# Convolution stage: the norm's shift, the partial sums and a scale are read from PSUM, and three more column groups are split

## The chip, the core and the metric

The kernel runs on one core of a Trainium2 chip. The metric is the device time of one execution in microseconds (us). An execution comprises a little more than the span of the profile, which goes from the first to the last instruction.

## The reference

One Conformer block and one sparse-attention block with an expert layer follow each other on 256 tokens of width 2048, all in float32. The change touches the first stage of the first block and the last norm of the second:

```python
h = rmsnorm(x, norm1_g)                      # x: 256 x 2048
u = h @ w_in + b_in                          # 2048 -> 2 x 2048
val, gate = split(u, 2)
u = val * sigmoid(gate)
u = causal_dwconv(u, dw) + dw_b              # 31 taps, one filter for each channel
u = silu(layernorm(u, ln_g, ln_b))
y = u @ w_out + b_out
...
h = layer_norm(ALPHA * h + ffn, ln2_g, ln2_b)    # the last operation of all
```

and, lightly, the gates of the expert layer, which are summed by products of one-hot matrices.

## The kernel before

Activations lie channel-major: a tile is 128 channels x 256 tokens, 16 such tiles make the width of 2048. Tiles of PSUM are 128x512 float32, one bank each; the pool has two tags of four banks, `mm` (sums of the large products) and `aux` (everything else).

**The convolution stage** is the loop over `o` from 0 to 15 (lines 472 to 509), where `o` stands for 128 channels of `val` and the 128 of `gate` that belong to them. For each `o` TensorE makes a group of products into two `mm` banks, in one of two forms. `whole` (line 358) takes the float32 weights as they are; each product shows as two matmul records in the profile, so a group is 64 records of L363. `halves` (line 365) takes weights that were split into a rounded high half `whi` (ScalarE, L132) and a remainder `wlo` (in this stage GpSimd, L121), with three matmuls in place of the two records: L373 and L374 read `whi`, L375 reads `wlo`, 96 records in all. A split costs four chunks of ScalarE and four of GpSimd. The tiles `wraw` have five buffers, `whi` and `wlo` four each, which is one group. The constant `WHOLE` lists the `o` that take the first form; 0 and 1 are made from unscaled data (`gx`) and scaled afterwards.

Then `ev_conv(o)` adds the bias, applies the gate (ScalarE L387, VectorE L388) and writes `u`. `do_conv(o)` runs the 31 taps over it, and three engines share them. The first `npool` taps are multiplied on ScalarE (L406, L409) and added up on GpSimd (L410). For `o` = 15 twelve taps are matmuls with diagonal matrices (L417). The rest run on VectorE as multiply-add (L433, L437) into two accumulators that take turns, so that an instruction does not wait for the one just before it. Each accumulator lies in a bank of its own. Three additions join the parts: L438 (the two accumulators), L440 (GpSimd's part `p`), L442 (TensorE's part). `npool` comes from `NPOOL`: 9 for an `o` in `WHOLE`, 7 for the others, with values of their own for 0, 1 and 15. The loop calls `do_conv(o - 1)` between the products of `o` and `ev_conv(o)`.

**The shift of the norm.** Once four tiles are convolved, `Layer.first` sums them with a matrix of ones (L306), ScalarE copies the negative mean to the SBUF tile `nm` (L308), and VectorE adds it to these four tiles (L310). For `o` >= 4 the shift is put in as the addend of the second VectorE tap. ScalarE squares each tile (L238), GpSimd adds up tiles and squares (L231), and after `o` = 15 small matmuls (L244) sum over channels.

**The scale before the stage.** The RMS scale is spread over partitions by a matmul into `rps`, ScalarE copies it to SBUF (`rB`, L469), and VectorE forms the 16 tiles of `h` (L471) from `x` and this copy. VectorE and GpSimd share the splitting of `h` into `A` (L121), which the `halves` groups read.

**The last norm** (lines 1230 to 1246) does the 16 tiles in pairs of 128x512, a multiplication and a subtraction each (L1239), with scales that ScalarE copied from PSUM to SBUF (L1234). VectorE has the pairs below `FINAL_POOL`, GpSimd the rest; ScalarE applies gain and offset (L1245), VectorE does so for the two tiles of `FINAL_DVE` (L1242).

**The gates** (`gate_prep`, `gate_fire`): 64 of them, each four products. The last two (n >= `SPLIT_FROM`) have a first operand split in two halves.

The order of the instructions on an engine is that of a planner which takes the program's order as priority and may move an instruction ahead where its operands are expected earlier; `tc.keep_in_program_order` and `tc.issue_after` fix some places.

Of the kernel before, what the change touches and what calls it, by code (L numbers as in the profile page):

```python
# [10 lines left out]
F32 = mybir.dt.float32  # L11
F32R = mybir.dt.float32r
# [3 lines left out]
OP = mybir.AluOpType  # L16
AX = mybir.AxisListType

T = 256
# [9 lines left out]
NM = 4  # L29
NPOOL = {'X': 9, 'Y': 7, 0: 7, 1: 7, 15: 5}  # L30
NPE = {15: 12}
DIAG_AT = 13
EARLY = 1
NGX = 2
FINAL_POOL = 10
FINAL_ORDER = (0, 2, 10, 4, 6, 12, 8, 14)
FINAL_DVE = (8, 9)
APOOL = 2
WHOLE = (0, 1, 3, 5, 7, 9, 11, 13, 15)
GATES_AT = 16  # L40
SPLIT_FROM = 62
PER_UNIT = 2.3
# [11 lines left out]
def tile_body(ctx: ExitStack, tc: tile.TileContext, xT, vec, dw, w_ccin, w_ccout, w_m1, w_m2,  # L54
# [7 lines left out]
    work = ctx.enter_context(tc.tile_pool(name="work", bufs=2))  # L62
    psum = ctx.enter_context(tc.tile_pool(name="psum", bufs=4, space=bass.MemoryType.PSUM))
    dram = ctx.enter_context(tc.tile_pool(name="dram", bufs=1, space=bass.MemoryType.DRAM))
# [16 lines left out]
    def aux(shape=None, name="aux"):  # L81
        return psum.tile(shape or [128, 512], F32, name=name, tag="aux", bufs=4)

    def bank():
        return psum.tile([128, 512], F32, name="mm", tag="mm", bufs=4)

    def wk(name, shape=None, dtype=F32, bufs=2, tag=None):
        return work.tile(shape or [128, T], dtype, name=name, tag=tag or name, bufs=bufs)
# [24 lines left out]
    def col(v, i):  # L113
        return vc[:, v + i:v + i + 1]
# [177 lines left out]
    class Layer:  # L292
# [7 lines left out]

        def first(self, o, ap):
            self.tiles.append(ap)
            if o == NM - 1:
                self.ps = aux()
                for i, t in enumerate(self.tiles):
                    PE.matmul(self.ps[:, :T], ones, t, start=i == 0, stop=i == NM - 1)  # L306
                self.nm = wk("nm", bufs=1)
                ACT.activation(self.nm, self.ps[:, :T], AF.Copy, scale=-1.0 / (128 * NM))  # L308
                for t in self.tiles:
                    DVE.tensor_tensor(t, t, self.nm, OP.add)  # L310
                    self.st.add(t)
# [78 lines left out]
    def do_conv(o):  # L390
        if o == NM:
            for i in range(NM):
                ln.first(i, conv[:, i])
        u = us[o % 3]
# [18 lines left out]
        if npe:  # L413
            pe = aux()
            for i in range(npe):
                k = npool + i
                PE.matmul(pe[:, :T], diag[o][:, i], u[:, k:k + T], start=i == 0, stop=i == npe - 1)  # L417
        acc = [aux(), aux()]
        y = conv[:, o]
        k0 = npool + npe  # L420
        for k in range(k0, 31):
            i = (k - k0) % 2
            d = acc[i][:, :T]
            a, b = w(k)
# [11 lines left out]
            else:  # L436
                DVE.tensor_scalar(d, a, b, None, op0=OP.mult)  # L437
        DVE.tensor_tensor(y, acc[1 - (30 - k0) % 2][:, :T], y, OP.add)  # L438
        if npool > 1:
            DVE.tensor_tensor(y, y, p, OP.add)  # L440
        if npe:
            DVE.tensor_tensor(y, pe[:, :T], y, OP.add)  # L442
        if o >= NM:
            ln.rest(y, shifted=True)
# [25 lines left out]
    for kt in range(KT):  # L470
        DVE.scalar_tensor_tensor(h[:, kt], x[:, kt], col(V_G1, kt), rB, op0=OP.mult, op1=OP.mult)  # L471
    for o in range(NGX):
# [6 lines left out]
    for o in range(NGX, KT):  # L479
# [27 lines left out]
        if o < EARLY:  # L507
            do_conv(o - 1)
    do_conv(KT - 1)
    lo_eng[0] = [POOL, DVE]  # L510
    ln.finish()
# [570 lines left out]
    def gate_prep(n):  # L1082

        if n >= SPLIT_FROM:
            o = [pk("oh", [128, 4, 128], F32R, tag=f"oh{i}", bufs=1) for i in range(3)]
            t = slice(4 * n, 4 * n + 4)
            ghi = pk("ghi", [128, 4], F32R, bufs=2)
            glo = pk("glo", [128, 4], bufs=2)
            ACT.activation(ghi, R[:, 2, t], AF.Copy)
            sub(DVE, glo, R[:, 2, t], ghi)  # L1090
            for i in range(4):
                t = slice(4 * n + i, 4 * n + i + 1)
                DVE.tensor_scalar(o[0][:, i], iota, R[:, 0, t], ghi.bitcast(F32)[:, i:i + 1], op0=OP.is_equal, op1=OP.mult)
                DVE.tensor_scalar(o[1][:, i], iota, R[:, 0, t], glo[:, i:i + 1], op0=OP.is_equal, op1=OP.mult)
                DVE.tensor_scalar(o[2][:, i], iota, R[:, 1, t], None, op0=OP.is_equal)
            gates[n] = o
            return
        if not spare:
# [11 lines left out]
    def gate_fire(n):  # L1110
        if n % 8 == 0:
            gs.append(slot(4 + n // 8 % 2, [128, 128, 32], name="gs"))
        *o1, o2 = gates.pop(n)
        ps = aux(wide4)
        for i in range(4):
            for j, a in enumerate(o1):
                PE.matmul(ps[:, i], a[:, i], o2[:, i], start=j == 0, stop=j == len(o1) - 1)  # L1117
        t = 4 * (n % 8)
        ACT.activation(gs[-1][:, :, t:t + 4].rearrange("p c t -> p t c"), ps, AF.Copy)  # L1119
        if n % 8 == 7:  # L1120
            nc.gpsimd.dma_start(Gd[n // 8], gs[-1])
# [113 lines left out]
    for kt in FINAL_ORDER:  # L1235
        y = z[:, kt:kt + 2]
        eng = DVE if kt < FINAL_POOL else POOL
        for w, op in zip(wide, (OP.mult, OP.subtract)):
            tc.keep_in_program_order(eng.tensor_tensor(y, y, w[:, None].to_broadcast([128, 2, T]), op))  # L1239
# [85 lines left out]
```

## Time and profile before

| | us |
|---|---|
| median of 3 runs (lowest to highest) | 3055.45 (3045.72 to 3058.11) |
| profiled execution, its own time | 3056.73 |
| its span | 3054.9 |
| TensorE (PE in the rows) busy in it | 2997.2 (98%) |
| VectorE (DVE) busy | 2138.3 (70%) |
| ScalarE (ACT) busy | 1576.6 (52%) |
| GpSimd (POOL) busy | 458.3 (15%) |

PEld in the rows is TensorE's loading of weights, which runs beside its matmuls. TensorE is busy almost throughout, so the shares of the whole span say little on a stage: GpSimd's 15% lie mostly in the first 230 us, where it is nearly full. The convolution stage fills the first 245 us or so and the last norm the last 20. Everything between is large products and is not touched, but for two of the 64 gates.

### The profile page before, as it was taken

Reading aid. Unit: us, or ns where it says so; the run is one execution under the profiler, and the core shown is the slowest. Engines: PE = TensorE matmul, PEld = TensorE weight load, DVE = VectorE, ACT = ScalarE, POOL = GpSimd, SP = SyncE. Lnnn points to the kernel's source line nnn. Section 1 sums busy time; section 2 is a strip of 40 time slices with the busy share of each in tenths; the row PEclk is TensorE's granted clock in tenths of the full one; section 3 lists DMA queues with packets and bytes.
Section 4 is the critical chain, followed back from the end, with each engine's and each line's share of the span. In section 5 each row is a group of like instructions: output and inputs, shape, how many; then the busy total and the mean of one; then the engine's idle time right before and its main releaser. Section 6 shows DMA issues by size and latency. Waiting matters only on the chain.

```text
span 3054.9 us, 47026 instructions
## 1 busy us (share of the span) xinstructions
PE 2997.2 (98%) x17614; PEld 2642.9 (87%) x17614; DVE 2138.3 (70%) x3892; ACT 1576.6 (52%) x2435; POOL 458.3 (15%) x554
## 2 busy tenths in 40 slices
PE   8998999999999999999999999999999999999997
PEld 7997888888888888898888888888888888888886
DVE  7997666455565876767899666666456667676765
ACT  4446554444444644565555555555555445454444
POOL 6883100000000120014400000000100000000014
PEclk9998999999999999999999999999999999999998
DMA  6443655555555555445456666666777777777663
GB/s 224 154 152 113 206 186 186 187 186 187 186 186 186 186 187 182 158 147 179 159 187 214 207 214 227 228 214 215 277 262 245 244 231 243 233 236 241 213 188 109
DMA packets 165045, 608.20 MB, mean 199 GB/s; under 512 B 18232, under 2 KB 20288, under 8 KB 163536
## 3 DMA queue, kind: packets, MB, share of 16 engines
q1 hardware_dynamic: 148992, 533.79, 52.7%
q0 software_dynamic: 15824, 71.41, 7.0%
q8 instruction: 137, 2.24, 0.3%
q14 instruction: 92, 0.75, 0.1%
HBM read 569.40 MB, written 37.24 MB: 199 GB/s over the span
## 4 chain that ended last, share of the span: by engine, by line
PE 91%; DVE 6%; POOL 1%; ACT 1%; issue 0%; DMA 0%; ACTq 0%; DVEq 0%; POOLq 0%
PE mm L145 54%; PE mm L146 28%; DVE aux L433 3%; PE aux L1117 2%; PE mm L363 2%; PE mm L820 0%; PE mm L818 0%; PE mm L819 0%; POOL hf L762 0%; DVE h L471 0%; DVE hf L1239 0%; PE mm L949 0%; PE mm L951 0%; DVE conv L440 0%; PE mm L950 0%
## 5 line engine op out<-in xcount | busy, mean ns | idle before, releaser
L145 PE MATMUL mm<-A,whi 128*128 128x512 f32 x7056 | 2484.3, 396 | 3.6 <-DVE A L121 3.4
L146 PE MATMUL mm<-A,wlo 128*128 128x256 f32 x7088 | 1986.8, 280 | 3.5 <-POOL wlo L121 1.9
L121 DVE TENSOR_TENSOR wlo<-wraw,whi 128x1024 fp32r<-128x1024 f32 x928 | 1139.8, 1233 | 783.7 <-ACT whi L132 782.7
L145 PEld LDWEIGHTS mm<-A,whi 128*128 128x128 f32 x7056 | 1324.0, 188 | 314.6 <-DVE A L121 4.2
L132 ACT ACTIVATE whi<-wraw 128x1024 fp32r<-128x1024 f32 x976 | 1029.6, 1057 | 1042.3 <-PE mm L145 767.4
L146 PEld LDWEIGHTS mm<-A,wlo 128*128 128x128 f32 x7088 | 1339.6, 189 | 4.9 <-POOL wlo L121 2.3
L183 ACT ACTIVATE cross<-mm 128x256 f32<-128x256 f32 x439 | 164.4, 374 | 89.8 <-PE mm L146 89.8
L121 POOL TENSOR_TENSOR wlo<-wraw,whi 128x1024 fp32r<-128x1024 f32 x48 | 117.7, 2463 | 56.1 <-ACT whi L132 56.0
L433 DVE SCALAR_TENSOR_TENSOR aux<-front,dwt,aux 128x256 f32<-128x256 f32 x314 | 125.1, 477 | 0.1
L1141 POOL DMA_DIRECT2D Ad<-staged x32 | 17.2, 536 | 628.2 <-ACT staged L1137 605.7
L1149 POOL DMA_DIRECT2D gt<-Gd x32 | 28.9, 904 | 499.6 <-DVE got L1162 447.4
L231 POOL TENSOR_TENSOR accq<-sq 128x256 f32<-128x256 f32 x5 | 3.9, 777 | 650.8 <-ACT sq L238 650.8
L1137 ACT ACTIVATE staged<-nrm 128x256 f32<-128x256 f32 x128 | 53.1, 415 | 90.7 <-DVE nrm L190 90.7
L363 PE MATMUL mm<-h,raw 128*128 128x256 f32 x448 | 98.0, 379 | 0.0
L190 DVE TENSOR_TENSOR nrm<-mm,cross 128x256 f32<-128x256 f32 x192 | 80.3, 418 | 22.4 <-ACT cross L183 22.4
L363 PEld LDWEIGHTS mm<-h,raw 128*128 128x128 f32 x448 | 84.8, 191 | 11.3
L1119 ACT ACTIVATE gs<-aux 128x512 f32<-128x512 f32 x64 | 72.8, 1138 | 26.8 <-PE aux L1117 26.8
L410 POOL TENSOR_TENSOR nr<-nr 128x256 f32<-128x256 f32 x106 | 78.9, 744 | 18.1 <-ACT nr L409 12.0
L145 PE MATMUL mm<-M,whi 128*128 128x512 f32 x224 | 79.3, 397 | 0.0
L231 POOL TENSOR_TENSOR accq<-sq,accq 128x256 f32<-128x256 f32 x64 | 59.5, 930 | 129.8 <-ACT sq L238 129.5
L146 PE MATMUL mm<-M,wlo 128*128 128x256 f32 x256 | 72.5, 283 | 2.6 <-DVE wlo L121 2.6
L373 PE MATMUL mm<-A,whi 128*128 128x256 f32 x224 | 65.6, 293 | 3.3 <-DVE front L382 2.3
(308 smaller groups left out, 2503.5 us busy)
## 6 DMA issues: line engine op xcount, KB each, us to landing
wraw<-w_m SPq DMA_DIRECT2D x256, 512.0 KB, 3.5
wraw<-w_u SPq DMA_DIRECT2D x256, 512.0 KB, 3.7
wraw<-w_v SPq DMA_DIRECT2D x256, 512.0 KB, 4.3
wraw<-w_p SPq DMA_DIRECT2D x80, 512.0 KB, 3.5
wraw<-w_ccin SPq DMA_DIRECT2D x36, 512.0 KB, 3.6
wraw<-w_ccout SPq DMA_DIRECT2D x32, 512.0 KB, 4.2
wraw<-w_o SPq DMA_DIRECT2D x32, 512.0 KB, 4.3
wraw<-w_q SPq DMA_DIRECT2D x32, 512.0 KB, 3.6
```

The source lines that it names most:

```text
L121: return eng.tensor_tensor(out_, a, b, OP.subtract)
L132: ACT.activation(hi[:, :, :m], raw[:, :, :m], AF.Copy)
L145: PE.matmul(ps, hi[:, k, cs], a, start=kt == 0, stop=False)
L146: PE.matmul(ps[:, :T], lo[:, k, cs], a[:, 0], start=False, stop=kt == KT - 1)
L183: ACT.activation(c, ps[:, T:], AF.Copy)
L190: return DVE.tensor_tensor(dst, ps[:, :T], c, OP.add)
L231: POOL.tensor_tensor(d, ap, self.acc[k], OP.add)
L363: PE.matmul(hold[j][:, :T], raws[c][:, k, blk(j)], src[:, kt], start=kt == 0, stop=kt == KT - 1)
L373: PE.matmul(d, hi[:, k, blk(j)], a[:, 0], start=kt == 0, stop=False)
L410: POOL.tensor_tensor(t, t, p, OP.add)
L433: DVE.scalar_tensor_tensor(d, a, b, add, op0=OP.mult, op1=OP.add)
L1119: ACT.activation(gs[-1][:, :, t:t + 4].rearrange("p c t -> p t c"), ps, AF.Copy)
```

## The change

It does eight things.

1. `NPOOL` goes from 9 to 8 for an `o` in `WHOLE` and from 7 to 5 for the others.
2. 5, 9 and 13 leave `WHOLE`, so that these groups are split (`halves`) and have 5 taps on GpSimd in place of 9.
3. The shift `nm` lies in a PSUM bank of its own and is written by VectorE.
4. The two accumulators of a convolution are the two halves of one bank. During the stage `aux` has three banks, the shift one, `mm` four; after the stage this pool is closed and one like that of before is opened.
5. The closing additions run in another order: TensorE's part first, then the two accumulators into the PSUM accumulator, then that plus GpSimd's part. None has two SBUF operands.
6. `h` is formed with the scale read from `rps` in PSUM; the copy `rB` stays for the first two groups.
7. The split form of the last two gates is gone; they take the form of the other 62.
8. In the last norm VectorE has six pairs in place of five and reads its scales from PSUM; GpSimd has two in place of three; the two tiles of `FINAL_DVE` are 10 and 11, and their pair comes last.

```diff
-NPOOL = {'X': 9, 'Y': 7, 0: 7, 1: 7, 15: 5}
+NPOOL = {'X': 8, 'Y': 5, 0: 7, 1: 7, 15: 5}
-FINAL_POOL = 10
-FINAL_ORDER = (0, 2, 10, 4, 6, 12, 8, 14)
-FINAL_DVE = (8, 9)
+FINAL_POOL = 12
+FINAL_ORDER = (0, 2, 12, 4, 6, 14, 8, 10)
+FINAL_DVE = (10, 11)
-WHOLE = (0, 1, 3, 5, 7, 9, 11, 13, 15)
+WHOLE = (0, 1, 3, 7, 11, 15)
-SPLIT_FROM = 62
...
-    psum = ctx.enter_context(tc.tile_pool(name="psum", bufs=4, space=bass.MemoryType.PSUM))
+    front_psum = tc.tile_pool(name="psum0", bufs=4, space=bass.MemoryType.PSUM)
+    psum = [front_psum.__enter__(), 3]
...
-        def first(self, o, ap):
+        def first(self, o, ap, nm=None):
...
-                self.nm = wk("nm", bufs=1)
-                ACT.activation(self.nm, self.ps[:, :T], AF.Copy, scale=-1.0 / (128 * NM))
+                if nm is None:
+                    self.nm = wk("nm", bufs=1)
+                    ACT.activation(self.nm, self.ps[:, :T], AF.Copy, scale=-1.0 / (128 * NM))
+                else:
+                    self.nm = nm
+                    DVE.tensor_scalar(nm, self.ps[:, :T], -1.0 / (128 * NM), None, op0=OP.mult)
...
+            nm = psum[0].tile([128, T], F32, name="nmp", tag="nmp", bufs=1)
...
-        acc = [aux(), aux()]
+        both = aux()
+        acc = [both[:, :T], both[:, T:]]
...
-        DVE.tensor_tensor(y, acc[1 - (30 - k0) % 2][:, :T], y, OP.add)
-        if npool > 1:
-            DVE.tensor_tensor(y, y, p, OP.add)
         if npe:
             DVE.tensor_tensor(y, pe[:, :T], y, OP.add)
+        other = acc[1 - (30 - k0) % 2]
+        DVE.tensor_tensor(other if npool > 1 else y, other, y, OP.add)
+        if npool > 1:
+            DVE.tensor_tensor(y, other, p, OP.add)
...
-        DVE.scalar_tensor_tensor(h[:, kt], x[:, kt], col(V_G1, kt), rB, op0=OP.mult, op1=OP.mult)
+        DVE.scalar_tensor_tensor(h[:, kt], x[:, kt], col(V_G1, kt), rps[:, :T], op0=OP.mult, op1=OP.mult)
...
     do_conv(KT - 1)
+    front_psum.__exit__(None, None, None)
+    psum[:] = ctx.enter_context(tc.tile_pool(name="psum", bufs=4, space=bass.MemoryType.PSUM)), 4
...
-        for w, op in zip(wide, (OP.mult, OP.subtract)):
+        for w, op in zip((p[:, :T] for p in lnf.po) if eng is DVE else wide, (OP.mult, OP.subtract)):
```

Left out are the removed branch of `gate_prep` and the loop over the two halves in `gate_fire`.

## Rows read from the trace of the kernel before

**Rows 1.** One stretch: length; busy PE, PEld, DVE, ACT, POOL; clock; DMA share, GB/s.

```profile
29.20:228.40 199.20, 192.55 (x1178) 178.53 (x1176) 191.99 (x414) 98.82 (x194) 174.11 (x166) 0.98 0.48 167
```

**Rows 2.** Groups in the first 260 us: busy us, mean ns | idle before, releaser.

```profile
L433 DVE SCALAR_TENSOR_TENSOR aux<-front,dwt,aux 128x256 f32<-128x256 f32 x314 | 125.1, 477 | 0.1
...
L410 POOL TENSOR_TENSOR nr<-nr 128x256 f32<-128x256 f32 x106 | 78.9, 744 | 18.1 <-ACT nr L409 12.0
L121 POOL TENSOR_TENSOR wlo<-wraw,whi 128x1024 fp32r<-128x1024 f32 x30 | 73.1, 2455 | 9.6 <-ACT whi L132 9.5
...
L433 DVE SCALAR_TENSOR_TENSOR aux<-front,dwt,nm 128x256 f32<-128x256 f32 x12 | 16.6, 1385 | 0.0
L440 DVE TENSOR_TENSOR conv<-conv,nr 128x256 f32<-128x256 f32 x16 | 14.4, 903 | 0.4
L471 DVE SCALAR_TENSOR_TENSOR h<-x,vc,nm 128x256 f32<-128x256 f32 x16 | 13.5, 914 | 1.2 <-ACT nm L469 1.2
...
L310 DVE TENSOR_TENSOR conv<-conv,nm 128x256 f32<-128x256 f32 x4 | 2.5, 690 | 0.2 <-ACT nm L308 0.2
```

**Rows 3.** Two additions, one line each: duration in ns, min/median/max.

```profile
L440 DVE TENSOR_TENSOR conv<-conv,nr x16: 407/644/2524, 59.8 to 240.1; 128x256 f32<-128x256 f32 x16
...
L438 DVE TENSOR_TENSOR conv<-aux,conv x16: 404/408/425, 59.1 to 239.6; 128x256 f32<-128x256 f32 x16
```

**Rows 4.** TensorE in order of time: start, us, instructions [idle before, released by].

```profile
42.16 0.35 PE L373 MATMUL mm<-A,whi 128*128 128x256 f32 x1 [2.31 <-DVE front L382]
...
55.86 0.58 PE L375 MATMUL mm<-A,wlo 128*128 128x256 f32 x1 [3.40 <-POOL wlo L121]
...
74.52 0.47 PE L373 MATMUL mm<-A,whi 128*128 128x256 f32 x1
...
86.23 13.97 PE L363 MATMUL mm<-h,raw 128*128 128x256 f32 x64
...
214.59 13.98 PE L363 MATMUL mm<-h,raw 128*128 128x256 f32 x64
234.02 7.67 PE L417 MATMUL aux<-front 128*128 128x256 f32 x24 [5.45 <-DVE front L388]
...
241.53 0.50 PE L244 MATMUL aux<-ones,accs 128*128 128x1 f32 x4
241.90 0.58 PE L244 MATMUL aux<-ones,accq 128*128 128x1 f32 x4
```

**Rows 5.** VectorE in order of time.

```profile
206.27 0.47 DVE L433 SCALAR_TENSOR_TENSOR conv<-front,dwt,aux 128x256 f32<-128x256 f32 x1
206.77 0.42 DVE L438 TENSOR_TENSOR conv<-aux,conv 128x256 f32<-128x256 f32 x1
...
233.48 0.48 DVE L388 SCALAR_TENSOR_TENSOR front<-mm,vc,front 128x256 f32<-128x256 f32 x1 [0.85 <-ACT front L387]
```

**Rows 6.** Two stretches after TensorE stood still, columns as in rows 1.

```profile
56.00:60.00 4.00, 4.00 (x19) 4.00 (x20) 4.00 (x12) 1.96 (x3) 3.61 (x6) 0.50 0.42 138
...
234.00:239.00 5.00, 4.98 (x13) 4.03 (x14) 5.00 (x13) 2.20 (x5) 2.90 (x4) 0.54 0.01 2
```

**Rows 7.** The last norm in order of time.

```profile
3037.57 0.38 ACT L1234 ACTIVATE accs<-aux 128x256 f32<-128x256 f32 x1 [0.53 <-PE aux L284]
...
3043.86 1.71 POOL L1239 TENSOR_TENSOR hf<-hf,nm 128x512 f32<-128x512 f32 x1
...
3047.83 0.69 DVE L1239 TENSOR_TENSOR hf<-hf,accs 128x512 f32<-128x512 f32 x1
3048.43 0.68 DVE L1239 TENSOR_TENSOR hf<-hf,nm 128x512 f32<-128x512 f32 x1
3048.55 3.06 ACT L1245 ACTIVATE hf<-hf,vc 128x256 f32<-128x256 f32 x6 [1.31 <-DVE hf L1239]
```

**Rows 8.** The gates' products, both forms: duration in ns, min/median/max.

```profile
L1117 PE MATMUL aux<-hot x320: 270/275/275, 1746.1 to 2163.5; 128*128 128x128 f32 x160
...
L1117 PE MATMUL aux<-oh x16: 222/274/280, 2184.9 to 2193.6; 128*128 128x128 f32 x16
```

More of the change, by code (lines that the diff above doesn't have):

```diff
@@ L81, in aux @@
     def aux(shape=None, name="aux"):
-        return psum.tile(shape or [128, 512], F32, name=name, tag="aux", bufs=4)
+        return psum[0].tile(shape or [128, 512], F32, name=name, tag="aux", bufs=psum[1])
     def bank():
-        return psum.tile([128, 512], F32, name="mm", tag="mm", bufs=4)
+        return psum[0].tile([128, 512], F32, name="mm", tag="mm", bufs=4)
     def wk(name, shape=None, dtype=F32, bufs=2, tag=None):
@@ L391, in do_conv @@
         if o == NM:
+            nm = psum[0].tile([128, T], F32, name="nmp", tag="nmp", bufs=1)
             for i in range(NM):
-                ln.first(i, conv[:, i])
+                ln.first(i, conv[:, i], nm)
         u = us[o % 3]
@@ L422, in do_conv @@
             i = (k - k0) % 2
-            d = acc[i][:, :T]
+            d = acc[i]
             a, b = w(k)
@@ L1082, in gate_prep @@
     def gate_prep(n):
[L1084 to L1097, printed above, removed]
         if not spare:
@@ L1112, in gate_fire @@
             gs.append(slot(4 + n // 8 % 2, [128, 128, 32], name="gs"))
-        *o1, o2 = gates.pop(n)
+        o1, o2 = gates.pop(n)
         ps = aux(wide4)
         for i in range(4):
-            for j, a in enumerate(o1):
-                PE.matmul(ps[:, i], a[:, i], o2[:, i], start=j == 0, stop=j == len(o1) - 1)
+            PE.matmul(ps[:, i], o1[:, i], o2[:, i], start=True, stop=True)
         t = 4 * (n % 8)
```

## The prediction

> **What bounds the kernel now.** I read the whole page first: TensorE is busy 98% of the span, so a change helps only where TensorE waits, works at the low clock or has work taken away. The change sits in two places, so I went on to the stretch from 29 to 228 us, the convolution stage [rows 1]. There three engines are nearly full: TensorE 192.6 of 199.2 us, VectorE 192.0, GpSimd 174.1 (87%). ScalarE, at 98.8, is half idle and covers its 12 further casts and 29 fewer multiplications. The groups of that stage [rows 2] show where VectorE's time goes. A tap with its addend in PSUM lasts 477 ns, and 314 of them fill 125.1 us, 0.398 us each. The same instruction with the addend `nm` in SBUF lasts 1385 ns on the mean. L440 and L471, which also have two tensor inputs in SBUF, have means of 903 and 914 ns, and L440 goes from 407 to 2524 ns [rows 3]; L438, the same addition with one input in PSUM, stays between 404 and 425. GpSimd runs additions and weight remainders from SBUF all that time, one remainder lasting 2455 ns [rows 2]. So the two-input instructions wait for GpSimd, and those with one input in PSUM do not.
>
> TensorE in order of time [rows 4] shows three stalls in the stage: 2.31 us for the freeing of its first banks, behind `h`; 3.40 us for a remainder; and 5.45 us ahead of the last diagonal products. [...] The last group ends at 214.59 + 13.98 = 228.57, and VectorE finishes its gating only after 233.48 [rows 5]: VectorE comes 4.9 us late, although the two are equally full.
>
> **The change, part by part.** *Operands moved to PSUM* (`h`, the shift, the closing addition). At 0.398 us each the 12 taps with the shift fall from 16.6 to 4.8 us, L471 from 13.5 to 6.4; at 0.41 each L440 from 14.4 to 6.6, L310 from 2.5 to 1.6 [rows 2, 3]. VectorE sheds 11.8 + 7.1 + 7.8 + 0.9 = 27.6 us. No row has exactly these operand pairs; the bounds are the SBUF rows (no gain) and the PSUM rows, and L433 is the same instruction, so I take the latter. The shift's copy changes engine: VectorE now waits for TensorE's sum itself where it waited for ScalarE; its taps stand behind it as before.
>
> [...] The shortest L440 (407) and the shortest L438 (404) say that a source in PSUM costs nothing extra [rows 3]. [...]
>
> *Taps from GpSimd to VectorE.* `NPOOL` and the three changed groups move 3 + 12 + 14 = 29 taps. VectorE gains 29 x 0.398 = 11.5 us, so over the stage it sheds 16.1, to about 176. GpSimd loses 29 x 0.744 = 21.6 us [rows 2].
>
> *Three groups split.* A `whole` group takes 13.97 us, a `halves` group 11.71 (74.52 to 86.23) [rows 4]. Three times 2.26 is 6.8 us less for TensorE. GpSimd gets 12 remainders of 2.455, 29.5 us. Its balance is +7.9, so 182.0 us. That it also waits less for VectorE is bounded by zero and 20 us (48 former collisions of one addition, 0.41); I take zero.
>
> *The head.* `h` done 7 us sooner frees the banks sooner: the 2.31 us go, as TensorE is then held by the group before. The 3.40 us came from a remainder queued on GpSimd behind the additions of the first convolution, which started late through the same `h`; they go too, and with them 2 us of four at half clock [rows 4, 6]. If the remainder stays late, 5.4 us of this stay.
>
> *The end of the stage.* TensorE alone would end at 228.57 - 2.31 - 3.40 - 2 - 6.8 = 214.1. GpSimd's 182.0 us, from 29.2, would end at 214.9 at 98% occupancy and 220.8 at 95%. VectorE's 176 us would end at 205, or 212 with the 7 us of waiting it has now. GpSimd is thus the next bound. I take it at 96%, an end of 218.8, a gain of 9.8. It cannot be fuller, since four buffers hold one group only; that it is fuller than 87% rests on its present waits being mostly for ScalarE, 12.0 and 9.5 us [rows 2], which waits for buffers and taps of a pace that rises. VectorE's 4.9 us of lag shrink to about 0.9, one ScalarE and one VectorE instruction: another 4.0.
>
> Behind it come the 24 diagonal records, 7.67 us. With TensorE hardly idle before them the clock should stay up: 24 x 13.97/64 = 5.2, up to 2.4 less. The new order puts two dependent additions behind TensorE's part, 0.50 us each (206.27 to 206.77 [rows 5]), up to 1.0 more. I take 1.2 less. The new pool's first bank is one that the old stage freed early, or the sums L244 wait about 1 us; I take zero.
>
> *The last norm.* VectorE's first subtraction must wait for the end of ScalarE's copy at 3037.95 [rows 7], since the copy comes first in the program and reads the same bank. A pair without collision takes 0.60 (3047.83 to 3048.43) plus 0.72 (0.69 and the 0.03 of a dependent pair), 1.32 us: first pair at 3038.7, five more to 3045.3, the two tiles of L1242, at L438's 0.41 each, to 3046. GpSimd's two pairs, four instructions of 1.71 [rows 7], are done by 3044. ScalarE's 14 tiles at 3.06/6 = 0.51 end, with small waits, at 3046.3, where they end now at 3051.6: 5.3 us less. If these reads cost as much as the colliding ones, nothing is gained.
>
> *The gates.* A gate takes eight records in either form (16 for two, 320 for forty), 274 and 275 ns [rows 8]: no difference on TensorE, and VectorE loses a few instructions where TensorE sets the pace. Zero; if the two gates now queue for shared buffers, still under 1 us.
>
> **Sum.** 9.8 + 4.0 + 1.2 + 5.3 = 20.3. The profiled execution took 3056.7 (span 3054.9 and 1.8 around it), so 3036.4. It lies 1.3 above the median of the runs, to which the forecast is made: 3035.
>
> **Rivals.** *Every tap waits for the one before it.* The two accumulators now share a bank. If instructions on one bank are kept in order to the end of each, the turns are worth nothing and a tap costs 0.50, as a dependent pair does [rows 5], in place of 0.398. 391 taps less the 16 first ones make 38 us more. VectorE's 176 become 214; with 7 us of waits the last gating comes at 250, 17 later than now, and with 5.3 back from the last norm and one more for the last convolution the time is 3055 + 17 + 1 - 5 = 3068. It decides from about 0.075 us a tap, 28 us (the 8 that VectorE has spare and the 20 gained). Against it: the small sums L244 go into one bank one every 0.09 us (four from 241.53 to 241.90 [rows 4]) while one is still under way, so an engine need not wait for itself; but they are TensorE's, and no row has VectorE alternating within a bank. [...] Chance 0.12.
>
> *GpSimd takes the gain.* With the same kind of waits as now it reaches 90% only. Then 182/0.90 = 202 us, an end at 231; the three groups and the head are eaten by late remainders, TensorE stands before L375, and only VectorE's lag (L388 at 232.3, 1.2 less) and the last norm remain: 3055.4 - 6.5 = 3049. For it: the sum of GpSimd's work grows. Against: its waits are for others' pace. Chance 0.22.
>
> *TensorE sets the pace alone.* GpSimd waits less for VectorE than I count and the stage ends at 214.1: 14.5 + 4.0 + 2.4 + 5.3 = 26 less, 3029. Chance 0.13.
>
> **From this the numbers.** Forecast 0.50, rivals 0.12, 0.22 and 0.13, 0.03 for a reordering elsewhere. About 0.5% (15 us) is what a measurement tells from no change. Below 3040: the third rival and most of the forecast, 0.58. Above 3071: half of the first rival and the rest, 0.08. Between: 0.34. From 3026 (third rival, less 3 of scatter) to 3052 (second, plus 3) about 0.8 lie.
>
> **What would show it.** Right: L471 near 0.47 us each, no tap or closing addition over 0.6 us; no idle TensorE of 2 us at 42; 224 + 96 records of L373; L388 of `o` = 15 at about 220; a last norm 5 us shorter. GpSimd over 95% busy from 29 to 219. Wrong: taps spaced 0.50; idle time before L375 with GpSimd as releaser that sums to over 8 us; the last L388 after 228.

## The result and the profile after

The change makes the kernel slower: 3067.85 us median (3058.11 to 3075.25, 18 runs) against 3048.74 for the kernel before in runs beside it (18 runs), a ratio of 1.0058, 95% interval 1.0045 to 1.0070. The profiled execution took 3073.6 us (span 3071.4), 16.9 more than that of before. The forecast was 3035. Times of one kernel lie in clusters some 12 us apart (28 runs of the kernel before beside four of the experiments: 3042 to 3048 and 3054 to 3059); where that comes from is told below.

First the convolution stage of the changed kernel, the stretch of [rows 1]:

```profile
29.20:228.40 199.20, 188.07 (x1276) 177.98 (x1275) 174.10 (x429) 95.12 (x173) 169.73 (x142) 0.98 0.45 162
```

and its groups from 29 to 245 us, with shapes kept apart, columns as in [rows 2]:

```profile
L439 DVE SCALAR_TENSOR_TENSOR aux<-front,dwt,aux 128x256 f32<-128x256 f32 x342 | 137.9, 483 | 0.2
L121 POOL TENSOR_TENSOR wlo<-wraw,whi 128x1024 fp32r<-128x1024 f32 x42 | 99.5, 2401 | 7.0 <-ACT whi L132 6.9
...
L379 PE MATMUL mm<-A,wlo 128*128 128x256 f32 x320 | 92.0, 289 | 8.5 <-POOL wlo L121 8.5
...
L392 DVE SCALAR_TENSOR_TENSOR front<-mm,vc,front 128x256 f32<-128x256 f32 x14 | 6.7, 480 | 21.9 <-ACT front L391 21.9
...
L478 DVE SCALAR_TENSOR_TENSOR h<-x,vc,aux 128x256 f32<-128x256 f32 x16 | 6.4, 478 | 1.2 <-ACT nm L476 1.2
...
L439 DVE SCALAR_TENSOR_TENSOR aux<-front,dwt,nmp 128x256 f32<-128x256 f32 x12 | 5.8, 482 | 0.0
```

The operands did what was forecast: `h` takes 478 ns in place of 914, a tap with the shift 482 in place of 1385. Yet no engine is full any more. VectorE, 192.0 us busy before, is busy 174.1 and waits 21.9 us for the gatings L392 (7.6 before); TensorE waits 8.5 us for remainders (3.4 before). TensorE and VectorE in order of time show where:

```profile
133.22 0.48 PE L379 MATMUL mm<-A,wlo 128*128 128x256 f32 x1 [2.19 <-POOL wlo L121]
...
191.64 0.58 PE L379 MATMUL mm<-A,wlo 128*128 128x256 f32 x1 [4.93 <-POOL wlo L121]
...
213.29 13.98 PE L367 MATMUL mm<-h,raw 128*128 128x256 f32 x64
228.35 5.45 PE L422 MATMUL aux<-front 128*128 128x256 f32 x24 [1.08 <-DVE front L392]
...
247.57 0.98 PE L244 MATMUL aux<-ones,accs 128*128 128x1 f32 x4 [13.77 <-DVE conv L449]
...
254.94 2.07 PE L284 MATMUL aux<-sq,ones 128*128 128x256 f32 x4 [2.12 <-DVE sq L282]
```

```profile
203.10 0.48 DVE L392 SCALAR_TENSOR_TENSOR front<-mm,vc,front 128x256 f32<-128x256 f32 x1 [9.30 <-ACT front L391]
...
227.81 0.48 DVE L392 SCALAR_TENSOR_TENSOR front<-mm,vc,front 128x256 f32<-128x256 f32 x1 [2.15 <-ACT front L391]
...
247.00 0.42 DVE L449 TENSOR_TENSOR conv<-aux,nr 128x256 f32<-128x256 f32 x1
```

The last group ends at 227.26 (228.57 before), the last gating comes at 227.81 (233.48 before), and still VectorE is done only at 247.0 and the spread of the norm's scales, L284, starts at 254.94. That start (246.39 in the kernel before) is the mark by which the stage is compared below. Two kernels with one and the same stage differ by 2 to 3 us in it.

While TensorE waited 13.77 us the granted clock fell to 0.50 and stayed there until about 266 us (windows, columns as in [rows 1]):

```profile
240.00:244.00 4.00, 0.00 (x0) 0.00 (x0) 3.93 (x9) 0.00 (x0) 0.00 (x0) 0.50 0.34 123
...
264.00:268.00 4.00, 4.00 (x18) 3.45 (x17) 4.00 (x14) 4.00 (x11) 3.67 (x6) 0.69 0.00 0
```

From there to the last gate the two kernels run 8.5 us apart. In the last stage of the experts, 785 us of nothing but pairs of a 512-column product (L145) and a 256-column one (L146), the distance grows again. These are the windows of L145 alone, that is one record for each pair, in two stretches of 600 us, in the changed kernel and then in the kernel before (columns: length, busy PE with the number of records, PEld, clock, DMA share, GB/s):

```profile
2300.00:2900.00 600.00, 600.00 (x1699) 319.12 (x1698) 1.00 0.69 233
455.00:1055.00 600.00, 600.00 (x1699) 319.12 (x1698) 1.00 0.53 186
```

```profile
2300.00:2900.00 600.00, 600.00 (x1732) 323.69 (x1731) 1.00 0.72 237
455.00:1055.00 600.00, 600.00 (x1699) 319.10 (x1699) 1.00 0.57 186
```

At the full clock in all four, 600 us hold 1699 pairs (353.1 ns each) or 1732 (346.4). TensorE never waits in these stretches; the pairs have two paces. The earlier stretch runs at the slow one in both profiles, the later one only in the changed kernel: 785 us at 6.7 ns a pair are 14.9 us. The last 153 pairs, behind that stage, go the other way (117 of them in 40 us in the changed kernel, 114 in the kernel before) and give 1.0 us back. It is not the profiled execution alone: none of the 18 runs of the changed kernel is under 3058 us, and 10 of the 18 of the kernel before are under 3051.

The last norm, in order of time:

```profile
3058.95 1.27 POOL L1233 TENSOR_TENSOR hf<-hf,nm 128x512 f32<-128x512 f32 x1 [12.84 <-ACT nm L1228]
...
3059.34 0.38 ACT L1228 ACTIVATE accs<-aux 128x256 f32<-128x256 f32 x1 [0.54 <-PE aux L284]
3059.76 7.28 DVE L1233 TENSOR_TENSOR hf<-hf,aux 128x512 f32<-128x512 f32 x11 [0.23 <-ACT accs L1228]
...
3061.80 6.00 ACT L1239 ACTIVATE hf<-hf,vc 128x256 f32<-128x256 f32 x12 [0.23 <-DVE hf L1233]
```

From the second copy to the end of the span it takes 3071.4 - 3059.34 = 12.1 us; before, 3054.9 - 3037.57 = 17.3 [rows 7]. The difference is 5.3, as forecast.

### The profile page after: what moved, and what is told of

The parts are those of the page before. It is cut to its first block, busy times and chain, and to the rows that moved or that the text cites. A ratio compares the mean times of both kernels' runs of the same rounds, so it can differ in the third digit from the quotient of the medians.

```text
span 3071.4 us, 47191 instructions
## 1 busy us (share of the span) xinstructions
PE 3006.7 (98%) x17710; PEld 2645.3 (86%) x17710; DVE 2120.8 (69%) x3914; ACT 1573.5 (51%) x2415; POOL 456.2 (15%) x535
## 4 chain that ended last, share of the span: by engine, by line
PE 90%; DVE 2%; POOL 1%; ACT 1%; issue 0%; DVEq 0%; ACTq 0%; POOLq 0%
PE mm L145 55%; PE mm L146 28%; PE aux L1111 2%; PE mm L829 0%; PE mm L827 0%; PE mm L828 0%; POOL hf L771 0%; DVE aux L439 0%; PE mm L367 0%; PE aux L244 0%; DVE wlo L121 0%; PE mm L958 0%; PE mm L142 0%; PE mm L143 0%; PE mm L379 0%
## 5 line engine op out<-in xcount | busy, mean ns | idle before, releaser
L145 PE MATMUL mm<-A,whi 128*128 128x512 f32 x7056 | 2498.7, 399 | 3.4 <-DVE A L121 3.4
L146 PE MATMUL mm<-A,wlo 128*128 128x256 f32 x7088 | 1989.4, 281 | 2.9 <-DVE wlo L121 1.6
L145 PEld LDWEIGHTS mm<-A,whi 128*128 128x128 f32 x7056 | 1326.6, 188 | 326.2 <-DVE A L121 4.2
L132 ACT ACTIVATE whi<-wraw 128x1024 fp32r<-128x1024 f32 x988 | 1042.1, 1057 | 1086.3 <-PE mm L145 776.7
L146 PEld LDWEIGHTS mm<-A,wlo 128*128 128x128 f32 x7088 | 1340.2, 189 | 4.2 <-DVE wlo L121 2.0
L121 POOL TENSOR_TENSOR wlo<-wraw,whi 128x1024 fp32r<-128x1024 f32 x60 | 143.4, 2413 | 52.8 <-ACT whi L132 52.7
L439 DVE SCALAR_TENSOR_TENSOR aux<-front,dwt,aux 128x256 f32<-128x256 f32 x343 | 138.4, 483 | 0.2
L379 PE MATMUL mm<-A,wlo 128*128 128x256 f32 x320 | 92.0, 289 | 8.5 <-POOL wlo L121 8.5
L377 PE MATMUL mm<-A,whi 128*128 128x256 f32 x320 | 93.3, 292 | 1.5 <-DVE front L392 1.5
L378 PE MATMUL mm<-A,whi 128*128 128x256 f32 x320 | 91.7, 287 | 0.0
L145 PE MATMUL mm<-M,whi 128*128 128x512 f32 x224 | 80.2, 402 | 0.0
L146 PE MATMUL mm<-M,wlo 128*128 128x256 f32 x256 | 72.8, 284 | 2.6 <-DVE wlo L121 2.6
L379 PEld LDWEIGHTS mm<-A,wlo 128*128 128x128 f32 x320 | 62.6, 196 | 9.2 <-POOL wlo L121 9.2
```

What stands on the lines that cost most here:

```text
L121: return eng.tensor_tensor(out_, a, b, OP.subtract)
L132: ACT.activation(hi[:, :, :m], raw[:, :, :m], AF.Copy)
L145: PE.matmul(ps, hi[:, k, cs], a, start=kt == 0, stop=False)
L146: PE.matmul(ps[:, :T], lo[:, k, cs], a[:, 0], start=False, stop=kt == KT - 1)
L377: PE.matmul(d, hi[:, k, blk(j)], a[:, 0], start=kt == 0, stop=False)
L378: PE.matmul(d, hi[:, k, blk(j)], a[:, 1], start=False, stop=False)
```

## The experiments

All runs in one table. "Mark" is the start of L284 (L283 or L285 where lines moved); 246.4 is the kernel before, 254.9 the changed one. Each ratio is against runs of the kernel before on the same chip.

| kernel | mark, us | median, us | ratio (95% interval) |
|---|---|---|---|
| changed, split gates kept | 252.4 | 3047.9 | 1.0006 (0.9987 to 1.0026) |
| before, gates not split | 244.3 | 3068.0 | 1.0053 (1.0033 to 1.0073) |
| changed, last gate's products twice | 253.3 | 3070.0 | 1.0055 (1.0033 to 1.0078) |
| changed, one interruption later | 251.9 | 3049.9 | 1.0020 (1.0004 to 1.0036) |
| changed, split gates, one convolution at a time | 287.7 | 3080.9 | 1.0118 (1.0081 to 1.0156) |
| changed, split gates, half a convolution apart | 251.5 | 3045.9 | 1.0012 (0.9996 to 1.0028) |
| changed, split gates, two banks, shift in SBUF | 241.8 | 3045.4 | 0.9981 (0.9963 to 1.0000) |
| changed, split gates, two banks | 244.4 | 3043.5 | 0.9973 (0.9952 to 0.9993) |
| the same, taps as before | 251.4 | 3052.9 | 1.0010 (0.9990 to 1.0029) |
| before, accumulators in one tile | 244.6 | 3051.1 | 0.9995 (0.9974 to 1.0015) |
| operands alone | 235.2 | 3041.5 | 0.9987 (0.9964 to 1.0011) |
| operands alone, again | 235.3 | 3041.2 | 0.9979 (0.9957 to 1.0001) |
| operands, one group more split | 240.8 | 3034.6 | 0.9963 (0.9940 to 0.9986) |
| operands, 13 taps moved | 238.0 | 3032.2 | 0.9948 (0.9929 to 0.9966) |
| operands, accumulators in one tile | 239.1 | 3043.2 | 0.9974 (0.9955 to 0.9993) |

**The gates.** The first theory was that the gates' form costs 15 us through the pace of the last stage. One kernel undoes that part, one does it alone:

```diff
+SPLIT_FROM = 62          # changed kernel: gate_prep and gate_fire as before
```

> The changed kernel with one part undone: the last two gates in their split form again. Theory (the pace of the last stage): in the last 785 us the changed kernel spends 353.4 ns on each pair of a 512-column and a 256-column product, the kernel before 346.7, and what sets the pace is what the last gate leaves behind. Then the pairs are back at 346.7 ns, 2220 pairs give back 14.7 us, and the time is 3068 - 15 = 3053 us. Rival (the gates cost nothing, as forecast, and the slower pairs come from elsewhere, such as the PSUM banks that the second pool gets): pairs stay at 353.4 ns, 3068 us.

```diff
-SPLIT_FROM = 62          # kernel before: gate_prep and gate_fire as changed
```

> The kernel before with that one part alone: the last two gates in the same form as the other 62. Theory (pace of the last stage): pairs after the last gate at 353.4 ns in place of 346.7, so 3048.7 + 14.7 = 3063 us, with the convolution stage unchanged. Rival (gates cost nothing): 3049 us, pairs at 346.7.

Both came as the theory has it. The pairs of the last stage with the split form back, and then without it in the kernel before (the 512-column product is L146 and L144 there):

```profile
2340.00:2900.00 560.00, 560.00 (x1617) 302.06 (x1616) 1.00 0.72 234
```

```profile
2300.00:2900.00 600.00, 600.00 (x1699) 319.06 (x1698) 1.00 0.71 233
```

That is 346.3 ns a pair with the split form and 353.1 without. By the ratios each kernel moves by some 16 us (from 1.0058 to 1.0006, and from 1 to 1.0053), and 15 of them are this stage; the medians move by 20 and 23, since they also depend on how many runs fall into which cluster. What about these gates sets the pace? Two kernels add products to the changed one:

```diff
             PE.matmul(ps[:, i], o1[:, i], o2[:, i], start=True, stop=True)
+        if n == 63:
+            for i in range(4):
+                PE.matmul(ps[:, i], o1[:, i], o2[:, i], start=True, stop=True)
```

> The changed kernel with nothing undone; the four products of the last gate are made a second time, with the same result (eight records more, about 1.1 us of work). Theory (the number of small products since the last change sets the pace: with each gate the pace goes one step on in a turn of three, slow, quick, quick, and the last gate ends on slow): one step on, the last stage's pairs take 346.7 ns, and the time is 3068 + 1.1 - 14.7 = 3054 us although more work is done. Rival (the form of the gates' products sets it): pairs stay at 353.4, 3069 us.

```diff
+        def mid(c):
+            if c == 2:
+                ps = aux(wide4)
+                for i in range(4):
+                    PE.matmul(ps[:, i], ident, ident, start=True, stop=True)
...
-        group(w_v[b, g], wts[b], ev, g, b == 7 and g == 7, lnf.st.early if b == 7 and g == 7 else None)
+        group(w_v[b, g], wts[b], ev, g, b == 7 and g == 7, lnf.st.early if b == 7 and g == 7 else mid if (b, g) == (0, 1) else None)
```

> The changed kernel with four small products (128 x 128, operands both the identity, result never read) between two pairs of the last stage's second group. Making the last gate's products twice in a row left the pairs at 353.3 ns. Theory (each interruption of the pairs by other products moves the pace one step on in the turn slow, quick, quick, however many products it holds): pairs behind the four products take 346.7 to 347 ns, 14 us less in all: 3054 us. Rival (only products of the split form's kind set the pace back): 353.3 to the end, 3069 us.

Products made twice in a row changed nothing (1699 pairs in 600 us), so their number does not decide. The same number at another place, between pairs, did; L145 before and behind the four products at about 2331 us:

```profile
2210.00:2330.00 120.00, 120.00 (x341) 63.88 (x340) 1.00 0.78 267
2335.00:2935.00 600.00, 600.00 (x1731) 324.49 (x1732) 1.00 0.71 232
```

351.9 ns a pair ahead of them, 346.6 behind: with more work the kernel is quicker, by 18 us at the median and by 12 by the ratios (1.0020 against 1.0058), and some 12 is what the 1807 pairs behind 2331 us give. So with these products it is the interruption that moves the pace on, and its place in a turn that says to which. The 64 gates show the turn: behind one the pairs take 353, behind the next 346.7, behind the third 346.9, and again, in both kernels; the last gate in the common form ends on 353. The split form does not end quickly by itself: in the run with the operands and one tile (below) it is there, and 560 us hold 1586 pairs (353.1 ns), since the turn had started one step off. Both runs fit if each of the two split gates moves the turn on by two steps where a common one moves it by one: behind the last two common gates and the two split ones the pairs take 353, 346.7, 353 and 346.7 ns in the kernel before (from the gate at 2171 us on), and 346.7, 346.7, 346.7 and 353 in that run (from 2150 on). No run tries this by itself.

**The shared tile.** Each accumulator gets a bank again; the bank is taken from the shift in the first kernel, and in the second three banks serve two convolutions:

```diff
-        both = aux()
-        acc = [both[:, :T], both[:, T:]]
+        acc = [aux()[:, :T], aux()[:, :T]]
```

> The changed kernel with the split gates back, the two accumulators in banks of their own again, and the shift in SBUF again (its bank is needed). Theory (the shared tile makes the planner interleave two convolutions, and that loses the stage): one convolution at a time, the last closing addition before 242 us (before: 242, changed: 247), 3053 - 8.5 - (0 to 8) = 3037 to 3045 us. Rival (the 29 taps moved to VectorE and the three split groups lose it, whatever the order): last closing addition still at 246 or later, 3050 to 3055 us.

> The changed kernel with the split gates back and the two accumulators of a convolution in banks of their own, out of the three banks there are; the shift stays in PSUM. So everything of the change is there but the shared bank and the gates. Theory (the shared tile alone made the stage long): with the shift in SBUF TensorE was through its last group at 217.1 us and VectorE came 9.9 us late; with the shift in PSUM VectorE saves 11.4 us on 12 taps and 3.4 on four additions, so the lag goes, the diagonal products start before 222 us, the pairs before 249 us (253 with the shift in SBUF, 256 in the kernel before), total 4 to 7 us less than with the shift in SBUF: 3030 to 3041 us. Rival (GpSimd sets the pace as soon as VectorE is quicker): pairs from 252 us on, no less than with the shift in SBUF.

The mark moves from 252.4 to 241.8 and 244.4, so the shared tile costs about 9 us here, with the 2 to 3 us by which the mark scatters. The second run missed its expectation: with the shift in PSUM the stage is not quicker. TensorE is through its last group at 218.80 and then waits:

```profile
204.82 13.98 PE L368 MATMUL mm<-h,raw 128*128 128x256 f32 x64
229.56 8.24 PE L423 MATMUL aux<-front 128*128 128x256 f32 x24 [10.77 <-DVE front L393]
```

The groups of that run, 29 to 229 us, say for whom. VectorE's closing additions L449 wait 14.3 us in all for GpSimd's sums:

```profile
L416 POOL TENSOR_TENSOR nr<-nr 128x256 f32<-128x256 f32 x73 | 54.0, 742 | 17.8 <-ACT nr L415 14.5
...
L449 DVE TENSOR_TENSOR conv<-aux,nr 128x256 f32<-128x256 f32 x14 | 5.9, 419 | 14.4 <-POOL nr L416 14.3
```

The 14.5 us for which the sums in their turn wait for ScalarE are not the cause: they lie elsewhere, 8.40 of them at 220.27, behind the last of the five waits of L449. Ahead of each of these five GpSimd works almost without a break, and remainders stand before the sums. The last one, GpSimd and then VectorE in order of time:

```profile
193.87 9.51 POOL L122 TENSOR_TENSOR wlo<-wraw,whi 128x1024 fp32r<-128x1024 f32 x4
203.32 0.75 POOL L416 TENSOR_TENSOR nr<-nr 128x256 f32<-128x256 f32 x1
...
206.08 2.24 POOL L416 TENSOR_TENSOR nr<-nr 128x256 f32<-128x256 f32 x3
```

```profile
207.67 0.42 DVE L449 TENSOR_TENSOR conv<-aux,nr 128x256 f32<-128x256 f32 x1 [2.39 <-POOL nr L416]
```

So the rival holds: GpSimd sets the pace.

How does one tile cost time? By the planner's dependences a tap now waits for the one before it, since both write one tile. VectorE's rows show how the planner avoids this: it takes taps of two convolutions in turn, with both gatings ahead. In the changed kernel runs of 41 and 44 taps follow two gatings (from 121.56 and 205.06 us), where in the kernel before 19 or 21 follow one. Two kernels force other orders with `tc.issue_after`:

```diff
+            with tc.issue_after(behind_conv[-1].ins) if k < k0 + 2 and behind_conv else ExitStack():
                 DVE.scalar_tensor_tensor(d, a, b, add, op0=OP.mult, op1=OP.add)
...
+        behind_conv.append(DVE.tensor_tensor(other if npool > 1 else y, other, y, OP.add))
```

> The changed kernel with the split gates back and with the first two taps of each convolution queued on VectorE behind the closing addition of the one before; the accumulators still share a bank. So each tap follows the tap whose result it waits for by the planner's dependences. Theory 1 (the planner's order alone makes the stage long; VectorE is not slowed by a shared bank): taps stay 0.39 us apart, the last closing addition comes at 230 to 240 us, total 3053 - 8.5 - (0 to 9) = 3036 to 3044 us. Theory 2 (a tap that waits for the one before it costs 0.50 us, and the planner's interleaving of two convolutions is what hid it): taps 0.50 apart, about 400 of them 44 us longer, of which VectorE's 22 us of idle time take up half: 3070 to 3090 us.

```diff
+            with tc.issue_after(half[-1].ins) if k < k0 + 2 and half else ExitStack():
...
+            if k == (k0 + 31) // 2:
+                half_next = tap
+        half.append(half_next)
```

> The changed kernel with the split gates back and the shared tile kept, and the first two taps of a convolution queued on VectorE behind the middle tap of the one before: two convolutions by turns, but half a convolution apart, as the order of the kernel before has them when its accumulators share a tile. Theory (what costs is that both gatings of a pair stand ahead of both convolutions, so that two whole convolutions lie behind the last gating): last tap within 12 us of the last gating (18.7 in the changed kernel), pairs from 254 to 258 us (264 with the split gates alone), total 3040 to 3045 against 3048 to 3053. Rival (the shared tile costs by itself, taps waiting for the tap before): pairs from 262 us on, taps over 0.45 us apart in more than a fifth.

One convolution at a time costs what the first rival of the prediction feared. VectorE in order of time, 19 taps:

```profile
152.39 9.94 DVE L443 SCALAR_TENSOR_TENSOR aux<-front,dwt,aux 128x256 f32<-128x256 f32 x19
```

That is 0.52 us a tap where the changed kernel has 0.39, and the mark moves by 35 us. Half a convolution apart, on the other hand, brought nothing (251.5 against 252.4): TensorE's last group ends 5 us earlier, at 219.8, but the wait for the last gating behind it grows from 1.1 to 11.9 us. My theory that the two gatings ahead are what costs fell; its rival holds by half, for the full-clock pairs start at 262.2 us, but a tenth of the taps lie over 0.45 us apart and not a fifth. GpSimd in order of time shows what the turns do elsewhere. The changed kernel, and then the one with two banks:

```profile
122.03 8.82 POOL L415 TENSOR_TENSOR nr<-nr 128x256 f32<-128x256 f32 x11
130.81 18.95 POOL L121 TENSOR_TENSOR wlo<-wraw,whi 128x1024 fp32r<-128x1024 f32 x8
```

```profile
112.96 3.17 POOL L416 TENSOR_TENSOR nr<-nr 128x256 f32<-128x256 f32 x4
116.08 2.37 POOL L122 TENSOR_TENSOR wlo<-wraw,whi 128x1024 fp32r<-128x1024 f32 x1
...
119.78 3.20 POOL L416 TENSOR_TENSOR nr<-nr 128x256 f32<-128x256 f32 x4
...
124.33 7.16 POOL L122 TENSOR_TENSOR wlo<-wraw,whi 128x1024 fp32r<-128x1024 f32 x3
```

Two convolutions in turn ask for the sums of two (4 + 7) at once; they go in one block, and eight remainders follow in another, while TensorE waits for the first of them. Two of the three waits that make the 8.5 us are of this kind, 2.19 us at 133.22 and 4.93 at 191.64. Apart, sums and remainders alternate, and TensorE waits 1.4 us for remainders in all. The same edit in the kernel before and in the one with the operands alone:

```diff
-        acc = [aux(), aux()]
+        both = aux()
+        acc = [both[:, :T], both[:, T:]]
```

> The kernel before with one edit: the two accumulators of a convolution are the halves of one tile. Theory (the planner, not the bank, loses the stage): taps of two convolutions by turns, 0.39 us apart, the pairs after the stage start 5 to 14 us later than the 256 us of the kernel before, 3054 to 3063 us in all. Rival (the interleaving costs only with the taps and groups that were moved): pairs from 256 us, 3049 us.

> The operands alone, with the two accumulators in one tile. With it the kernel before lost nothing (pairs from 255.9 us against 255.8), the changed kernel some 8 us (264 against 255.7). Theory 1 (the turns of two convolutions cost where VectorE's order sets the end of the stage, whatever the groups): pairs from 248 to 254 us against 243.9. Theory 2 (they cost only where the remainders of the split groups are late): pairs from 242 to 246 us.

By the mark, without the three split groups one tile costs nothing in the kernel before (244.6 against 246.4 and, with unsplit gates, 244.3) and 3.9 us with the operands alone (239.1 against 235.2). The expectations name another point, the first pair at the full clock's spacing. By that the kernel before loses nothing either (256.0 against 255.8 us), but the operands alone lose 5.9 (249.9 against 244.0), which lies in the range of theory 1 and not of theory 2; 100 pairs further on it is 2.5 (284.4 against 281.9). So one tile is dearer with the split groups, about 9 us, and part of its price comes without them; the two theories are not told apart. That the blocks on GpSimd are the cause of the rest is argued from these rows, not shown.

**Groups, taps, operands.** From the kernel with two banks the taps go back, and then the groups too, which leaves the operands, the closing order and the last norm:

```diff
-NPOOL = {'X': 8, 'Y': 5, 0: 7, 1: 7, 15: 5}
+NPOOL = {'X': 9, 'Y': 7, 0: 7, 1: 7, 15: 5}
```

> The same, and the 29 taps back on GpSimd (nine and seven taps a convolution, as in the kernel before), with the three more groups split. Theory: GpSimd, 171 of 188 us busy in the stage with the taps away, gets 21.6 us more and becomes the bound: the remainders come late, pairs start at 255 to 262 us, total 3045 to 3055. Rival (GpSimd's idle time absorbs them): within 3 us of the run without them.

```diff
-WHOLE = (0, 1, 3, 7, 11, 15)
+WHOLE = (0, 1, 3, 5, 7, 9, 11, 13, 15)
```

> The kernel before with the operands alone: the scale, the shift and the closing additions from PSUM, and the new last norm; taps, groups, gates and separate accumulators as before. Theory (the three more split groups put 12 more casts on ScalarE ahead of its multiplications, GpSimd's additions come late and VectorE's closing additions wait for them, 14 us in the run with everything but the bank and the gates): without the groups that wait is under 4 us, the last gating comes by 226 us, the pairs start by 250 us (256 before), total 5 for the last norm and 5 to 10 for the stage under the kernel before, ratio 0.995 to 0.997. Rival (the stage holds nothing to gain, since VectorE's lag grows again): pairs from 253 to 256 us, ratio 0.998 to 0.999.

The last two kernels differ in the three groups, with the six taps that a split group has less on GpSimd (100 sums in place of 106), and the mark by 16.1 us. The taps that the first of them moves back are thus 23 and not 29 (77 sums in the kernel with two banks). With the groups split, GpSimd is busy 179.2 of the 188.8 us from 29.2 to 218, TensorE waits for it, and so does VectorE (groups, 29 to 234 us):

```profile
L380 PE MATMUL mm<-A,wlo 128*128 128x256 f32 x320 | 93.1, 291 | 14.1 <-POOL wlo L122 14.1
...
L449 DVE TENSOR_TENSOR conv<-aux,nr 128x256 f32<-128x256 f32 x14 | 5.9, 420 | 26.3 <-POOL nr L416 26.2
```

With the operands alone the stage goes as the working had it. TensorE in order of time:

```profile
206.48 13.98 PE L368 MATMUL mm<-h,raw 128*128 128x256 f32 x64
221.54 5.45 PE L423 MATMUL aux<-front 128*128 128x256 f32 x24 [1.09 <-DVE front L393]
...
235.22 2.07 PE L285 MATMUL aux<-sq,ones 128*128 128x256 f32 x4 [2.12 <-DVE sq L283]
```

Its last group ends at 220.46 without a stall from 70 us on, VectorE comes 1.1 us behind, and L449 waits 6.7 us for GpSimd. Three more, for the interval and for what may yet be had:

> The operands alone once more, for a narrower interval (its ten times lay from 3028 to 3056, on several levels some 12 us apart). Theory (the operands and the last norm together take 12 + 5 us off): ratio 0.994 to 0.997. Rival (only the last norm counts): 0.998.

```diff
-WHOLE = (0, 1, 3, 5, 7, 9, 11, 13, 15)
+WHOLE = (0, 1, 3, 5, 7, 11, 13, 15)       # and 'Y': 6
```

> The same with one more group split (o = 9) and the Y convolutions' share on GpSimd six taps in place of seven. Theory: one group's four casts still fit into ScalarE's and GpSimd's slack, TensorE has 2.3 us less, the pairs start 1 to 3 us before those of the run without. Rival (any cast ahead of the multiplications delays the closing additions): pairs 0 to 4 us later.

```diff
-NPOOL = {'X': 9, 'Y': 7, 0: 7, 1: 7, 15: 5}
+NPOOL = {'X': 8, 'Y': 6, 0: 7, 1: 7, 15: 5}
```

> The operands alone, with 16 of the taps moved from GpSimd to VectorE (eight and six a convolution in place of nine and seven). Theory (VectorE's closing additions wait 6.7 us for GpSimd's sums, so less work there shortens the wait, and VectorE has room): pairs 1 to 3 us before the 243.9 us of the run without, if TensorE, 186.7 of 188.8 us busy, leaves that much. Rival (TensorE sets the pace now): pairs within 1 us, or later by the 16 taps at 0.39 us, 6 us.

By the mark one group more split, with ten taps moved, costs 5.6 us, and the taps moved alone 2.8 (they are 13 and not 16: 93 sums in place of 106). Both come later, as the rivals have it, the first by more than the rival's 4. The operands alone have the shortest stage, 10 us under the kernel before. Yet both their ratios missed the expected range: 0.9987, and again 0.9979 with an interval that reaches 1.0001, as the rivals had it. That the two kernels with longer stages have better ratios is the clusters' doing (five of the six runs with the taps moved lie between 3031 and 3034): among profiled executions with the same pace from 455 to 1055 us the operands alone are ahead, with 3032.1 against 3034.5 (one more group) at the quick pace, and with 3039.3 against 3044.9 (taps moved) and 3056.7 (the kernel before) at the slow one. The two runs of the operands alone are one program. Their windows of L146 (which is L145 of the other kernels):

```profile
455.00:1055.00 600.00, 600.00 (x1732) 324.48 (x1732) 1.00 0.58 190
```

```profile
455.00:1055.00 600.00, 600.00 (x1700) 319.11 (x1699) 1.00 0.58 186
```

One execution runs the stretch quick (span 3030.3), the other slow (3037.5). The stretch alone is some 12 us; shorter ones behind it go the other way (from 1610 to 1680 us 199 and 201 pairs). TensorE waits for nothing from 258 to 1055 us in either, and both hold 228 pairs from 345 to 425; they part behind two records of L285 at 435.8. So here the pace behind an interruption is not the program's to choose, and going by these two executions that makes the clusters.

## Why the prediction was wrong

By the marks, the stage goes from 245.4 (kernel before, mean of two) to 235.2 with the operands, to 251.4 with three groups split, to 244.4 with 23 taps moved (the other six went with the groups), to 253.1 with one tile (mean of the four kernels that have that stage): -10.1, +16.1, -7.0, +8.8, together +7.8, where the forecast had -15.0. The gates add 14.9, of which the last 153 pairs give 1.0 back, and the last norm takes 5.3. The sum is +16.4; the profiles differ by 16.9, the medians by 19.1.

- *Operands moved to PSUM, the head, the diagonal products, the last norm:* right in mechanism and about right in size. 228.57 - 2.31 - 3.40 - 2 = 220.9 was TensorE's end without the three groups; it measured 220.46. Both waits of the head are gone, but that the sum is met to 0.4 us is luck: a wait of 2.06 us at 66.87 came in, and one of 0.94 at 51.96 went, and the forecast has neither. The diagonal products took 5.45 us (5.2 forecast), `h` 478 ns, the last norm 5.3 us less. On the price of a source in PSUM the forecast went by the rows, and they held: the closing addition with one operand in PSUM and one in SBUF takes 419 ns, where the shortest of two SBUF operands took 407 [rows 3], 12 ns less. That instructions with two SBUF operands waited for GpSimd shows again in the last norm of the kernel before: six of L1239 on VectorE, from 3037.98 to 3046.04, took 1.45 to 1.75 us beside GpSimd's, and the three behind the last of GpSimd's 0.68 or 0.69.
- *Three groups split* is the first step that failed. With two banks TensorE's last group ends at 218.80, where I had written 218.8, but that is luck: my number was GpSimd's end at 96%, and of the 6.8 us that TensorE was to save against the 220.46 without the groups 1.7 came (it waits 1.4 us for remainders, and its granted clock is 0.93 from 50 to 75 us). And "VectorE's 4.9 us of lag shrink to about 0.9" failed: the last gating comes at 229.0, 10.2 us behind. GpSimd was the bound, and it shows less as a late remainder than as late sums, for which VectorE's closing additions wait 14.3 us. In the changed kernel, with one tile, they wait 0.1 us, and the remainders are late instead (8.5 us). GpSimd at 96% was the choice; it reached 169.9 of 188.8 us, 90%, the figure of the rival in which it takes the gain, and 85% in the changed kernel.
- *One bank for the accumulators* was costed at nothing, with a rival for 0.50 us a tap. 3068, the rival's time, is what was measured, but by coincidence and not by its way: the taps stay 0.39 us apart, because the planner turned the order round, and one tile costs 8.8 us with the three groups split. Forced into one convolution at a time the taps take 0.52. The 0.52 come with a wait that the planner puts in, and a bank shared without it was not tried: the taps 0.39 apart belong to two convolutions in turn, so each goes to another bank than the one before it.
- *The gates: "no difference on TensorE ... Zero"* is the largest failure, 14.9 us. Their own records are alike, as [rows 8] say; what the forecast left out is the pairs behind them, 785 us of them.

Of the signs named, these held: L478 near 0.47, no closing addition over 0.6, no idle TensorE at 42, 320 records of the first products with the high halves, the last norm. These failed: the last gating at 227.81 in place of 220, GpSimd at 85% in place of 95, 8.5 us idle before the remainders' products.

## What to carry to other kernels

Where a stage has several nearly full engines, moving work costs where the next queue in order stands behind it: ask not whether the new instructions fit into the engine's idle time, but what waits for the last of them (here VectorE's closing additions for GpSimd's sums). Putting two buffers into one tile changes what the planner takes for dependent and may turn the order on every engine; compare the orders, and not only the durations. And after any edit ahead of a long uniform stretch compare the number of its instructions in a fixed window, for two per cent of 785 us are 15 us, more than any other part of this change gave.

## What the hardware showed that was not expected

Pairs of a 512-column and a 256-column product on a TensorE that never waits, at a granted clock of 1.00, run at one of two paces, 346.4 or 353.1 ns, and keep it for up to 785 us. The gates' products between them move it on in a turn of three (slow, quick, quick), eight records at one place as much as sixteen. Behind two other records, at 435.8 us, either pace came in one and the same program, 12 us apart over the stretch from 436 to 1070 us, although both executions had the same pace and no wait ahead of it. What in the chip sets it stays open: program, operands and granted clock are the same in both cases.
